# Sums of squares for an RMS norm: eight halves of tokens take another way, and one operand of a Strassen set is stored whole

## The chip, the cores and the metric

The kernel runs on one core of one Trainium2 chip. The metric is device time in microseconds (us) for one execution of the whole program; the time before is the median of three executions. TensorE (PE in the profile) multiplies matrices, VectorE (DVE), ScalarE (ACT) and GpSimd (POOL) do everything else, and SyncE (SP) issues nearly all the transfers (DMAs), in the order of its queue.

## The reference

Two layers over 1024 tokens of width 1024, in f32. Each layer is `h = h + mixer(rms_norm(h))` and then `h = h + conv_ffn(rms_norm(h))`; the first mixer is retention plus a gated delta rule, the second an RG-LRU; a last norm ends the program. What the change touches is the norm, which is computed five times:

```
def _rms(x):
    xf = x.astype(jnp.float32)
    return xf * lax.rsqrt(jnp.mean(xf * xf, axis=-1, keepdims=True) + EPS)
...
def conv_ffn(hn, w_up, conv_w, conv_b, w_down):
    up = causal_dwconv(hn @ w_up, conv_w) + conv_b
    gate, val = jnp.split(up, 2, axis=-1)
    return (jax.nn.silu(gate) * val) @ w_down
```

## The kernel before, in words

**Layout.** `h` lies in SBUF as eight tiles `H[m]` with 128 channels on the partitions and 1024 tokens along the free axis, and all work on it goes by halves of 512 tokens (n=0, n=1). The mean of squares of a token is therefore a sum over eight tiles and then over the 128 partitions.

**Products.** Weights and activations are split into a high and a low part in fp32r, and a product is three matmuls (lines 328 to 330: high by high, high by low, low by high). A weight quarter arrives by DMA into `raw` (7 buffers), is split by ACT (line 270, `whi`) and DVE (line 271, `wlo`) into a ring of 6 buffers, and a ring place comes free when TensorE has used it. So ACT and DVE can be up to 6 quarters ahead of TensorE, and no more.

**The norm.** `square_step` squares a half of each tile on ACT (line 416, the first one 407) and adds it to an accumulator on DVE (line 420); the eighth square is not added but kept beside it. `norm_tok` sums both over the partitions on TensorE: for each of the two arrays four f32 matmuls with one column of ones (line 433), in all eight, which leave one number per token, 128x4. Line 437 (DVE) scales it, line 438 (POOL) takes the power -0.5. `norm_row` turns it into a row on all partitions with four f32 matmuls of 128x128 (line 448); in three of the norms ACT copies that row from PSUM into `R` (line 451), in the others it is read from PSUM.

Where the halves are: the first norm stands at the start of the program (line 1518 on), while `x` is loaded. `down_x` (line 509) ends the first layer's FFN; its rows scale the projections of the RG-LRU (lines 388 and 1034). `down_pairs` (line 517) ends both mixers; as soon as a half is done, `pair_operands` builds from it, in small steps beside the next half's products, seven Strassen operands: scaled blocks (line 567, ACT), times the row (line 570, DVE), differences (594 and others), and high and low parts (583 and 587). For the second half these steps stand in a written order on DVE and ACT, and TensorE multiplies the first half's operands while they run (`pair_halves`). `final` (line 906) goes in three parts of 512, 256 and 256 tokens.

**The FFN's second matrix.** The hidden activations of 16 of the 22 pairs are multiplied by Strassen's seven products too, in two sets c=0 and c=1. `store_parts` writes four operands (0, 1, 3, 5) already split to `p_dram`, high and low, and three (2, 4, 6) whole to `s_dram`. `load_set` reads an operand back when TensorE has finished the one in its place: a split one with 8 DMAs straight to its place (line 831), a whole one with 4 DMAs into `t` (line 838), by way of six half-tile places that are used in turn, and is then split by ACT (line 840) and DVE (line 841). Set 0 is loaded while the last pair's products run.

**What sets the order.** The program is written in slots of three matmuls (`slot`, line 333); `steps` and `after` put an action so many slots later, so every `yield` of a generator is a slot. A scheduler then orders each engine's queue. Each engine runs its queue strictly in order: a waiting instruction holds everything behind it.

## Time and profile before

| what | before |
|---|---|
| median of 3 runs | 2199.09 us (2198.58 to 2200.04) |
| profiled execution, its own time | 2200.31 us |
| its span, first to last instruction | 2198.5 us |
| TensorE busy | 2176.4 us, 99% |
| VectorE busy | 1696.0 us, 77% |
| ScalarE busy | 1069.7 us, 49% |
| DMA bytes | 305.34 MB, 139 GB/s |

A busy TensorE is not one at its peak, since matmuls overlap: a 128x512 matmul shows 0.39 us, while the next starts 0.23 us later. So what an edit is worth on TensorE is read from start to start. An f32 matmul leaves two records, so the eight matmuls of a `norm_tok` show as x16.

### The profile page before, as it was taken

What the parts mean: (1) busy time and instruction counts of PE and PEld (TensorE: products, weight loads), DVE (VectorE), ACT (ScalarE), POOL (GpSimd) and SP (SyncE); (2) the same over time, 40 slices, a digit from 0 to 9 for tenths busy, and PEclk for the clock granted to TensorE, in tenths of its full rate; (3) what the DMA queues carried; (4) which work ended last, traced back from release to release, by engine and by line L of the source; (5) the groups of instructions that cost most, each with busy time, mean ns of one, the idle gap of its engine ahead of it and who ended that gap; (6) DMA issues with size and microseconds to landing.
All of it is one profiled execution on the core that took longest, in us unless ns stands there. A gap on an engine that the chain in (4) does not pass through costs nothing.

```text
span 2198.5 us, 29909 instructions
## 1 busy us (share of the span) xinstructions
PE 2176.4 (99%) x10844; PEld 1819.5 (83%) x10844; DVE 1696.0 (77%) x2576; ACT 1069.7 (49%) x1712; POOL 80.8 (4%) x73
## 2 busy tenths in 40 slices
PE   9999999999999999999999999999999999999998
PEld 8887888887888888887888888888888888878888
DVE  6988766446899988987865677778999889878644
ACT  5334433124565555554323476765655555544321
POOL 0100111200000000000000000000000000000001
PEclk9999999999999999999999999999999999999999
DMA  4243424125234544438546211242245445375542
GB/s 173 81 141 99 128 83 145 57 79 175 63 120 167 179 153 157 163 111 287 197 160 201 82 53 63 85 147 73 101 165 171 148 173 177 115 271 178 190 165 77
DMA packets 203300, 305.34 MB, mean 139 GB/s; under 512 B 31728, under 2 KB 91408, under 8 KB 203152
## 3 DMA queue, kind: packets, MB, share of 16 engines
q1 hardware_dynamic: 202720, 301.85, 40.7%
q8 instruction: 85, 1.39, 0.3%
q10 hardware_dynamic: 432, 1.58, 0.2%
q14 instruction: 63, 0.52, 0.1%
HBM read 212.63 MB, written 90.72 MB: 138 GB/s over the span
## 4 chain that ended last, share of the span: by engine, by line
PE 89%; DMA 4%; DVE 4%; issue 2%; ACT 1%; POOL 1%; SPq 0%; POOLq 0%; DVEq 0%; ACTq 0%
PE ps L328 27%; PE ps L330 27%; PE ps L329 27%; DMA t<-sf_dram 1%; DMA t<-y_dram 1%; PE pc L433 1%; DMA s<-pf_dram 1%; DMA h<-in_xT_dram 0%; DVE wlo L271 0%; PE pc L448 0%; DVE l L1273 0%; DVE l L1271 0%; PE pc L328 0%; PE pc L330 0%; PE pc L329 0%
## 5 line engine op out<-in xcount | busy, mean ns | idle before, releaser
L328 PE MATMUL ps<-s,whi 128*128 128x512 f32 (+1 forms) x2792 | 1091.0, 392 | 3.9 <-ACT s L840 1.8
L329 PE MATMUL ps<-s,whi 128*128 128x512 f32 (+1 forms) x2792 | 1084.5, 388 | 1.0 <-DVE s L841 0.7
L330 PE MATMUL ps<-s,wlo 128*128 128x512 f32 (+1 forms) x2792 | 1083.9, 388 | 0.0
L270 ACT CAST whi<-raw 128x512 fp32r<-128x512 f32 (+1 forms) x612 | 371.5, 613 | 659.1 <-PE ps L329 515.6
L328 PEld LDWEIGHTS ps<-s,whi 128*128 128x128 f32 x2792 | 524.9, 188 | 112.5 <-ACT s L840 3.1
L330 PEld LDWEIGHTS ps<-s,wlo 128*128 128x128 f32 x2792 | 524.7, 188 | 108.1 <-DVE wlo L271 0.3
L329 PEld LDWEIGHTS ps<-s,whi 128*128 128x128 f32 x2792 | 525.2, 188 | 107.3 <-DVE s L841 1.8
L271 DVE TENSOR_TENSOR wlo<-raw,whi 128x512 fp32r<-128x512 f32 (+1 forms) x612 | 412.9, 680 | 60.8 <-ACT whi L270 57.2
L774 DVE SCALAR_TENSOR_TENSOR t<-halo,cols,t 128x1024 f32<-128x1024 f32 x176 | 222.1, 1282 | 4.8 <-ACT t L772 3.5
L747 DVE TENSOR_TENSOR halo<-ps,kept 128x512 f32<-128x512 f32 (+1 forms) x138 | 92.2, 668 | 75.5 <-PE ps L330 74.2
L757 DVE TENSOR_TENSOR h<-ps,h 128x512 f32<-128x512 f32 x112 | 77.4, 691 | 82.2 <-PE ps L330 81.9
L772 ACT ACTIVATE t<-halo,cols 128x1024 f32<-128x1024 f32 x88 | 109.7, 1246 | 16.9 <-DVE halo L747 11.6
L742 ACT COPY kept<-ps 128x512 f32<-128x512 f32 (+1 forms) x138 | 77.0, 558 | 13.3 <-PE ps L330 11.2
L498 DVE TENSOR_TENSOR h<-ps,h 128x512 f32<-128x512 f32 (+1 forms) x72 | 45.3, 631 | 43.3 <-PE ps L330 43.3
L438 POOL TENSOR_TENSOR rtok<-rtok,npow 128x4 f32<-128x4 f32 (+1 forms) x11 | 11.2, 1016 | 1722.3 <-DVE rtok L437 1668.7
L857 DVE TENSOR_TENSOR t<-t 128x1024 f32<-128x1024 f32 x44 | 53.7, 1221 | 0.0
L797 ACT CAST t<-t 128x512 fp32r<-128x512 f32 x64 | 38.1, 620 | 32.0 <-DVE t L857 30.7
L852 ACT ACTIVATE t<-t 128x1024 f32<-128x1024 f32 x44 | 46.8, 1063 | 10.1 <-DVE t L774 10.0
L416 ACT ACTIVATE t<-h 128x512 f32<-128x512 f32 (+1 forms) x49 | 27.2, 562 | 46.3 <-DVE h L498 41.5
L840 ACT CAST s<-t 128x512 fp32r<-128x512 f32 x48 | 29.5, 621 | 38.4 <-DMA t<-sf_dram 34.0
L328 PE MATMUL ps<-s,s 128*128 128x256 f32 (+1 forms) x144 | 46.2, 321 | 0.0
L329 PE MATMUL ps<-s,s 128*128 128x256 f32 (+1 forms) x144 | 45.8, 318 | 0.0
(293 smaller groups left out, 2074.5 us busy)
## 6 DMA issues: line engine op xcount, KB each, us to landing
raw<-in_ffn_up_dram SPq DMA_DIRECT2D x176, 256.0 KB, 2.7
s<-pf_dram SPq DMA_DIRECT2D x128, 256.0 KB, 5.3
pf_dram<-t SPq DMA_DIRECT2D x64, 256.0 KB, 2.6
pf_dram<-lo SPq DMA_DIRECT2D x64, 256.0 KB, 2.5
sf_dram<-t SPq DMA_DIRECT2D x64, 256.0 KB, 2.2
t<-sf_dram SPq DMA_DIRECT2D x64, 256.0 KB, 5.0
raw<-in_ffn_w_dram SPq DMA_DIRECT2D x64, 256.0 KB, 2.9
raw<-in_mix_in_dram SPq DMA_DIRECT2D x62, 256.0 KB, 2.9
```

The lines of the kernel that those rows point to most:

```text
L270: self.nc.scalar.copy(hi[:, 0:w], raw[:, 0:w])
L271: eng.tensor_tensor(lo[:, 0:w], raw[:, 0:w], f32(hi[:, 0:w]), ALU.subtract)
L328: mm(ps, whi, xhi, start=start, stop=False)
L329: mm(ps, whi, xlo, start=False, stop=False)
L330: mm(ps, wlo, xhi, start=False, stop=stop)
L742: A.copy(kept[o], ps)
L747: V.tensor_tensor(dst(i, j), v(ps), v(kept[k]), ALU.add)
L757: V.tensor_tensor(h(*to[o]), ps.rearrange("p (h c) -> p h c", c=256), h(*to[o]), ALU.add)
L772: A.activation(t, buf[:, 2:2 + T], AF.Identity, scale=w(0), bias=self.col(f"ffn_cb{layer}", tile_i))
L774: V.scalar_tensor_tensor(t, buf[:, 2 + j:2 + j + T], w(j), t, ALU.mult, ALU.add)
L852: A.activation(tg, tg, AF.Silu)
L857: V.tensor_tensor(tg, tg, tv, ALU.mult)
```

## The change

1. With `st["whole"]`, the eighth square is added to the accumulator like the others, so `norm_tok` needs four matmuls for that half. This stands for both halves of the first norm, the second half of `down_x`, and the second part of `final` (256 tokens, two matmuls).
2. Four halves go by `norm_beside` and leave TensorE altogether: the first half of `down_x`, of both `down_pairs`, and the first part of `final`. DVE transposes the accumulator in blocks of 32x32 (`block_sums`) and reduces it to 128x16; four DMAs write these block sums to DRAM, one element at a time; a DMA reads them back by token, DVE adds the four, POOL takes the power, a DMA writes the row to DRAM and another reads it, broadcast, into `R`. All of these DMAs go by SP's queue.
3. In `pair_operands` the first half's row is now read from `R`; its steps start 16 slots after the last square, not 3, with no gap in them.
4. In the FFN, operand 5 of set 0 is stored whole (one DMA, straight from the activations) and split when it is loaded.

```diff
+        self.nsum = 0
...
-        if k == KT - 1:
+        if k == KT - 1 and not st.get("whole"):
             st["acc"].append(sq)
         else:
             nc.vector.tensor_tensor(st["acc"][0], st["acc"][0], sq, ALU.add)
+        if k == KT - 2:
+            st["free"] = sq
+
+    def block_sums(self, out, src, room):
+        self.nc.vector.transpose(room, src)
+        self.nc.vector.tensor_reduce(out, room.rearrange("p (b j) -> p b j", j=32), AX.X, ALU.add)
+
+    def norm_beside(self, st, n):
+        nc, V = self.nc, self.nc.vector
+        self.nsum += 1
+        sums = self.tc.dram_tile([4, HALF], F32, name=f"nsum_dram{self.nsum}")
+        row = self.tc.dram_tile([HALF], F32, name=f"nrow_dram{self.nsum}")
+        small = lambda name: self.sm.tile([P, 16], F32, tag=name, name=name, bufs=1)
+        b = small("nblk")
+        self.block_sums(b, st["acc"][0], st["free"])
+        for a in range(4):
+            nc.sync.dma_start(sums[a].rearrange("(b i) -> i b", i=32), b[32 * a:32 * a + 32, :])
+        x = small("ntok")
+        nc.sync.dma_start(x.rearrange("p (a c) -> p a c", a=4), sums.rearrange("a (p c) -> p a c", c=4))
+        r = self.sm.tile([P, 4], F32, tag="rtok", name="rtok")
+        V.tensor_reduce(r, x.rearrange("p (a c) -> p c a", a=4), AX.X, ALU.add)
+        V.tensor_scalar(r, r, 1.0 / D, EPS, ALU.mult, ALU.add)
+        nc.gpsimd.tensor_tensor(r, r, self.npow[:, 0:4], ALU.pow)
+        nc.sync.dma_start(row.rearrange("(p c) -> p c", c=4), r)
+        nc.sync.dma_start(self.R[:, n * HALF:(n + 1) * HALF], row.partition_broadcast(P))
+        self.has_row[n] = True
...
         def then(n, st, m, h):
+            st["whole"] = True
             self.square_step(st, m, self.norm_step(st, m, gain, n))
             if m == KT - 1:
-                self.steps((9, 7)[n], self.norm_rest(st, n, 3))
+                if n == 0:
+                    self.norm_beside(st, n)
+                else:
+                    self.steps(8, self.norm_rest(st, n, 3))
...
+            st["whole"] = n == 0
             self.square_step(st, m, h)
             if m == KT - 1:
+                if n == 0:
+                    self.norm_beside(st, n)
                 self.build[n] = self.pair_operands(st, n, gain, 4)
-                self.steps(3, self.build[n])
+                self.steps((16, 3)[n], self.build[n])
...
-        yield from self.norm_tok(st, wait=2)
+        if n == 0:
+            rows = self.R[:, 0:256], self.R[:, 256:HALF]
+        else:
+            yield from self.norm_tok(st, wait=2)
...
-        s_dram = self.tc.dram_tile([2, 4, 4, P, HALF], F32, name=f"sf_dram{layer}")
+        s_dram = self.tc.dram_tile([2, 5, 4, P, HALF], F32, name=f"sf_dram{layer}")
...
-        place = {1: 0, 4: 1, 2: 2, 6: 3}
-        whole = {0: 0, 1: 1, 3: 2, 5: 3}
+        place = {1: 0, 4: 1, 2: 2, 6: 3, 5: 4}
+        whole = [{0: 0, 1: 1, 3: 2}, {0: 0, 1: 1, 3: 2, 5: 3}]
...
-            store_split(5, v[:, :, 0], slice(HALF, T))
+            if 5 in whole[c]:
+                store_split(5, v[:, :, 0], slice(HALF, T))
+            else:
+                nc.sync.dma_start(halves(s_dram[c, place[5], k % 4]), v[:, :, 0])
...
-            st = {}
+            st = {"whole": t0 < 768}
...
-        s1 = part(512, 256, {2: [lambda: run(self.norm_tok(s0[0]))], 6: [lambda: run(self.norm_row(s0[0], 0))]})
+        self.norm_beside(s0[0], 0)
+        s1 = part(512, 256, {})
...
-            st, src = {}, {}
+            st, src = {"whole": True}, {}
```

**Where instructions move.** Line numbers of the changed kernel are higher: its 272, 400, 421 and 529 are the lines 271, 399, 420 and 498 of before, 468 and 479 are 437 and 448, and 608, 629 and 636 are 570, 587 and 594.

The first place is the first norm, on DVE, around the scaling of the first half's sums (`rtok<-pc`). Before:

```order
L420 TENSOR_TENSOR t<-t 128x512
L399 SCALAR_TENSOR_TENSOR s_96<-h_88,cols,s_96 128x512
L399 SCALAR_TENSOR_TENSOR s_96<-h_89,cols,s_96 128x512
L437 TENSOR_SCALAR rtok<-pc 128x4
L1177 TENSOR_SCALAR l_117<-l_117 128x4
L1601 TENSOR_SCALAR og<-cols 128x1
L399 SCALAR_TENSOR_TENSOR s_96<-h_90,cols,s_96 128x512
```

And now:

```order
L400 SCALAR_TENSOR_TENSOR s_96<-h_95,cols,s_96 128x512
L421 TENSOR_TENSOR t<-t 128x512
L468 TENSOR_SCALAR rtok<-pc 128x4
L421 TENSOR_TENSOR t<-t 128x512
L291 MEMSET wab 128x512 x2
L389 TENSOR_TENSOR halo_98<-ps,R 128x512
L389 TENSOR_TENSOR halo_99<-ps,R 128x512
L389 TENSOR_TENSOR l_117<-ps,R 128x512
L468 TENSOR_SCALAR rtok<-pc 128x4
```

The scaling of the first half has moved from behind the second half's second tile (`h_89`) to behind its last (`h_95`), and stands three rows ahead of the evacuations (`halo<-ps,R`) that need the row. On TensorE the row's matmuls have moved by as much: they now stand right ahead of the second half's `norm_tok`, and behind both come the first matmuls that need an evacuated bank.

The second place is the first `down_pairs`, behind the last tile (`h_95`) of its first half. DVE before:

```order
L498 TENSOR_TENSOR h_95<-ps,h_95 128x512
L271 TENSOR_TENSOR wlo<-raw,whi 128x512 x2
L437 TENSOR_SCALAR rtok<-pc 128x4
L498 TENSOR_TENSOR h_88<-ps,h_88 128x512
L271 TENSOR_TENSOR wlo<-raw,whi 128x512
L570 TENSOR_TENSOR t<-t,pc 128x1024 x2
L587 TENSOR_TENSOR s_4180<-t,s_4180 128x1024
```

DVE now, two rows further on (`h_88`, `h_89` and `h_90` are the first tiles of the second half):

```order
L529 TENSOR_TENSOR h_88<-ps,h_88 128x512
L272 TENSOR_TENSOR wlo<-raw,whi 128x512 x2
L446 TENSOR_REDUCE rtok<-ntok 128x4
L447 TENSOR_SCALAR rtok<-rtok 128x4
L529 TENSOR_TENSOR h_89<-ps,h_89 128x512
L272 TENSOR_TENSOR wlo<-raw,whi 128x512
L421 TENSOR_TENSOR halo_99<-halo_99 128x512
L272 TENSOR_TENSOR wlo<-raw,whi 128x512
L608 TENSOR_TENSOR t<-t,R 128x1024 x3
L629 TENSOR_TENSOR s_4174<-t,s_4174 128x1024
L529 TENSOR_TENSOR h_90<-ps,h_90 128x512
```

And SP's queue at the same place now; the rows other than 442 to 450 stood there before in the same order:

```order
L442 DMA nsum_dram_4777<-nblk 32x16x1 x4
L261 DMA raw<-in_mix_outb_dram 128x512
L261 DMA raw<-in_mix_outa_dram 128x512
L444 DMA ntok<-nsum_dram_4777 128x4x4
L261 DMA raw<-in_mix_outb_dram 128x512
L449 DMA nrow_dram_4778<-rtok 128x4
L302 DMA raw<-in_ffn_up_dram 128x512
L450 DMA R<-nrow_dram_4778 128x512
L302 DMA raw<-in_ffn_up_dram 128x512 x12
```

The build of the first half's operands, which began behind the addition to `h_88`, now begins behind that to `h_89`, and DVE stands twice for a DMA: at `rtok<-ntok` and at `t<-t,R`. Each DMA of the new chain has a weight load ahead of it in SP's queue.

The third place is SP's queue where set 0 is loaded. Before (the rows from the second to the sixth are operands 2, 3, 4, 5 and 6):

```order
L831 DMA s_4180<-pf_dram_5165 128x2x256 x6
L838 DMA t<-sf_dram_5164 128x512 x4
L831 DMA s_96<-pf_dram_5165 128x2x256 x8
L838 DMA t<-sf_dram_5164 128x512 x4
L831 DMA s_96<-pf_dram_5165 128x2x256 x8
L838 DMA t<-sf_dram_5164 128x512 x4
L301 DMA raw<-in_ffn_w_dram 128x512 x4
```

And now:

```order
L877 DMA s_4174<-pf_dram_5159 128x2x256 x6
L884 DMA t<-sf_dram_5158 128x512 x4
L877 DMA s_96<-pf_dram_5159 128x2x256 x8
L884 DMA t<-sf_dram_5158 128x512 x12
L302 DMA raw<-in_ffn_w_dram 128x512 x4
```

Operand 5's eight loads have become four, which go by the six places in `t` between those of operands 4 and 6, and four splits on ACT and on DVE have been added behind them.

More of the change, by code (lines that the diff above doesn't have):

```diff
@@ L140, in __init__ @@
         pad(self.perm, 104, "pad2")
-        pad(self.sm, 40, "pad3")
+        pad(self.sm, 24, "pad3")
         self.nhalo = 0
         self.npp = 0
+        self.nsum = 0
         self.lo_engine = nc.vector
@@ L575, in pair_operands @@
         scaled(b12, 0, 1)
-        yield from range(gap)
-        self.run(self.norm_row(st, apart=True))
-        rows = st["rows"]
+        if n == 1:
+            yield from range(gap)
+            self.run(self.norm_row(st, apart=True))
+            rows = st["rows"]
         place = lambda o: [self.operand(o)[:, n, e:e + 4, :] for e in (0, 4)]
@@ L799, in store_split @@
                 for e, t in enumerate((hi, lo)):
-                    nc.sync.dma_start(p_dram[c, whole[o], k % 4, e], f32(t[:, at]))
+                    nc.sync.dma_start(p_dram[c, whole[c][o], k % 4, e], f32(t[:, at]))
             store = lambda o, r: nc.sync.dma_start(s_dram[c, place[o], k % 4], r)
@@ L822, in store_parts @@
             store(6, t4)
-            store_split(5, v[:, :, 0], slice(HALF, T))
+            if 5 in whole[c]:
+                store_split(5, v[:, :, 0], slice(HALF, T))
+            else:
+                nc.sync.dma_start(halves(s_dram[c, place[5], k % 4]), v[:, :, 0])
         def load_set(c, o):
             x = self.operand(o)
-            if o in whole:
+            if o in whole[c]:
                 for k in range(4):
                     for e in range(2):
-                        nc.sync.dma_start(f32(x[:, :, 4 * e + k, :]), halves(p_dram[c, whole[o], k, e]))
+                        nc.sync.dma_start(f32(x[:, :, 4 * e + k, :]), halves(p_dram[c, whole[c][o], k, e]))
                 return
```

## The prediction, made before the changed kernel was run

> **What bounds the kernel now.** I read the page first, its busy times and the chain that ended last, then TensorE's timeline around the matmuls that the change removes, and then the windows in which TensorE waits.
>
> ```profile
> PE 2176.4 (99%) x10844; PEld 1819.5 (83%) x10844; DVE 1696.0 (77%) x2576; ACT 1069.7 (49%) x1712; POOL 80.8 (4%) x73
> PE 89%; DMA 4%; DVE 4%; issue 2%; ACT 1%; POOL 1%; SPq 0%; POOLq 0%; DVEq 0%; ACTq 0%
> 1215.67 0.39 PE L329 MATMUL ps<-s,whi 128*128 128x512 f32 x1
> 1215.90 0.39 PE L330 MATMUL ps<-s,wlo 128*128 128x512 f32 x1
> 1216.13 1.84 PE L433 MATMUL pc<-ones,t 128*128 128x1 f32 x16
> 1217.83 0.49 PE L328 MATMUL ps<-s,whi 128*128 128x512 f32 x1
> 1218.15 0.40 PE L329 MATMUL ps<-s,whi 128*128 128x512 f32 x1
> 1218.39 0.40 PE L330 MATMUL ps<-s,wlo 128*128 128x512 f32 x1
> ```
>
> TensorE carries 89% of the chain, and its matmuls start 0.23 us apart with nothing between. So whatever leaves its queue shortens the run by its own length, as long as no wait takes its place. What a `norm_tok` costs is read from start to start: 1217.83 - 1216.13 = 1.70 us, and the next two matmuls start 0.09 and 0.01 us later than the usual 0.23: 1.80 us for eight f32 matmuls.
>
> ```profile
> 550.95 0.94 PE L433 MATMUL pc<-ones,halo 128*128 128x1 f32 x8
> 551.76 0.49 PE L328 MATMUL ps<-s,whi 128*128 128x512 f32 x1
> 557.54 1.05 PE L448 MATMUL pc<-ident,rtok 128*128 128x128 f32 x8
> 558.35 0.48 PE L328 MATMUL ps<-s,whi 128*128 128x512 f32 x1
> ```
>
> Half a `norm_tok` is 0.81 + 0.10 = 0.91 us, and a row 0.81 + 0.09 = 0.90 us.
>
> **The change, part by part.** Four halves lose 1.80 + 0.90 = 2.70 us each, 10.8 us in all; three lose 0.90 and a quarter-sized one 0.40, 3.1 us in all. If nothing else moved, the program would be 13.9 us shorter. I go through the five places to see what of it is kept.
>
> *Both halves of `down_x`.* The first half's row isn't needed until the projections behind the second half, over 30 us later, so the DRAM way is covered. DVE's wait for the block sums holds back work there, but DVE is not full: 8.4 of 12 us (a window's columns are its length, the busy time of PE, weight loads, DVE, ACT and POOL, the clock, the DMA share and GB/s).
>
> ```profile
> 1204.00:1216.00 12.00, 12.00 (x55) 9.94 (x54) 8.37 (x15) 6.58 (x13) 0.00 (x0) 1.00 0.37 100
> 2140.00:2170.00 30.00, 30.00 (x216) 28.33 (x215) 10.80 (x20) 6.74 (x13) 2.81 (x3) 1.00 0.00 1
> ```
>
> I count the whole 2.70 + 0.90 = 3.6 us. *`final`* is as free: DVE works 10.8 of 30 us, DMA nothing. 2.70 + 0.40 = 3.1 us; what ends the program, the third part's norm, is not touched.
>
> *First norm.* Two halves of 0.90 us go. But the first half's scaling (468, before 437) now stands behind all of the second half's additions on DVE.
>
> ```profile
> 21.76 0.16 DVE L437 TENSOR_SCALAR rtok<-pc 128x4 f32<-128x4 f32 x1 [0.71 <-PE pc L433]
> 23.64 1.16 PE L448 MATMUL pc<-ident,rtok 128*128 128x128 f32 x8 [0.17 <-POOL rtok L438]
> 28.95 0.68 DVE L420 TENSOR_TENSOR t<-t 128x512 f32<-128x512 f32 x1
> 31.24 1.84 PE L433 MATMUL pc<-ones,t 128*128 128x1 f32 x16
> L451 ACT COPY R<-pc x2: 568/578/588, 27.7 to 41.7; 128x512 f32<-128x512 f32 x2
> L388 DVE TENSOR_TENSOR halo<-ps,R x4: 680/684/692, 29.6 to 46.4; 128x512 f32<-128x512 f32 x4
> ```
>
> DVE ends that addition at about 29.6 as before (one addition of 0.6 more, a wait of 0.71 less), and from the scaling to the row were 23.64 - 21.76 = 1.88 us: the row at 31.4. TensorE, which begins the second half's `norm_tok` at 31.24, would be there near 30.5 (six more matmuls ahead of it, 1.36, less 0.91, the old row's 0.90 and its wait of 0.34), so it waits 0.9 us; and since the evacuations need the row by way of ACT (0.58 us) and DVE (0.68 us), with only 0.8 us of `norm_tok` to cover them, it waits some 0.8 us again before it gets a bank. Of 1.8 us, and 0.34 us of the row's old wait, I keep 0.6; the bounds are 1.8 us won and 1 us lost.
>
> *First halves of the two `down_pairs`.* This is the place that decides. Before, the row came from TensorE, and DVE was full from 570 to 586 (the window in this fence is DVE's alone; its columns are length, busy, clock, DMA share, GB/s):
>
> ```profile
> 549.11 0.69 DVE L498 TENSOR_TENSOR h<-ps,h 128x512 f32<-128x512 f32 x1 [1.60 <-PE ps L330]
> 558.18 2.35 DVE L570 TENSOR_TENSOR t<-t,pc 128x1024 f32<-128x1024 f32 x2 [0.51 <-PE pc L448]
> 595.73 0.68 DVE L498 TENSOR_TENSOR h<-ps,h 128x512 f32<-128x512 f32 x1
> 597.87 0.95 PE L433 MATMUL pc<-ones,halo 128*128 128x1 f32 x8
> 570.00:586.00 16.00, 16.00 (x21) 1.00 0.18 54
> l_dram<-h SPq DMA_DIRECT2D x32, 16.0 KB, 1.5
> l<-t_dram SPq DMA_DIRECT2D x64, 16.0 KB, 1.9
> raw<-in_ffn_up_dram SPq DMA_DIRECT2D x176, 256.0 KB, 2.7
> L438 POOL TENSOR_TENSOR rtok<-rtok,npow 128x4 f32<-128x4 f32 x9 | 9.7, 1075 | 1707.4 <-DVE rtok L437 1653.9 <-DVE splq L1076 33.0 <-DVE og L1601 20.5
> L1354 DVE TENSOR_REDUCE ov<-l 128x4 f32<-128x512 f32 x16 | 11.0, 684 | 10.8 <-ACT l L1352 10.8
> L1246 SPq DMA_DIRECT2D l_dram<-h x32: 302/424/1571, 99.1 to 139.6; - x32
> DMA to landing us min/median/max: 1.4/1.5/4.2
> ```
>
> When is the new row in `R`? The last square is added near 551.3 (549.11, a square, an addition). No row shows a transpose; the reduce of the same 128x512 takes 0.68, and I take as much for each of the two: 552.7. Four issues of 512 single elements: 0.42 us for 128 pieces (`l_dram<-h`) is the lower bound; I take 0.6 each, 555.1. Landing 1.5 (upper bound 4.2), read back 1.9 and its issue, with a weight load between: 559. Two small DVE steps and the power (1.08): 560.7. Written behind another weight load, 1.5: 562.5. Broadcast behind a third, 2.7 as for another 256 KB: near 566. With every landing at 4.2 it is some 8 us later, with issues and landings at their least 3 us sooner.
>
> From there the changed order has on DVE 15 steps of 128x1024 (2.35 / 2 = 1.17 us) and 23 of 128x512 (0.6 us from start to start) before the addition to the second half's last tile: 15 x 1.17 + 23 x 0.6 = 31 us, so at 597 us, 1.3 later than the 595.73 of before. TensorE would have that tile ready at 592.7 (2.7 sooner), and its second-half `norm_tok` must wait. It had about 0.8 us in hand (597.87 against 595.73 and a square of 0.63), so it comes 0.5 to 0.7 us later than before, not 2.7 sooner: TensorE waits 3.4 us instead of working 2.7. I count 0.7 us lost in each, 1.4 in all. The bounds for each: 2.7 won, if the row comes 3 us sooner; 7 lost, if it comes 8 later.
>
> The wait has a second price. Where TensorE ran thin before, its clock was halved for a while:
>
> ```profile
> 1977.00:1979.00 2.00, 0.95 (x3) 0.48 (x3) 0.93 (x2) 0.86 (x2) 0.00 (x0) 1.00 1.05 403
> 1981.00:1983.00 2.00, 2.00 (x7) 1.52 (x6) 1.59 (x2) 2.00 (x4) 0.00 (x0) 0.50 0.09 34
> 1030.00:1040.00 10.00, 8.96 (x37) 6.09 (x35) 5.57 (x10) 3.90 (x7) 0.00 (x0) 1.00 1.07 392
> ```
>
> The third of these rows is a stretch nearly as thin that did not halve it. A clock of 0.50 for the 3 to 4 us seen there costs half of that, 1.7 us; I keep it in the range only. The Trainium skill's page "TensorE: Matmul & The Clock Gate", in its part 1 on the clock gate, says that the clock falls after an idle window of about 3.4 us. By that rule a wait of 3.4 us stands just at the edge, and the sum would be up to 3.4 us worse for both places; the row above disagrees in that the clock fell with three matmuls in two microseconds, without such an idle window.
>
> *Operand 5 of set 0, in both layers.* The windows from 1010 to 1050 show what it touches:
>
> ```profile
> 1010.00:1020.00 10.00, 10.00 (x46) 8.29 (x45) 6.56 (x10) 3.01 (x6) 0.00 (x0) 1.00 1.03 359
> 1040.00:1050.00 10.00, 9.56 (x38) 6.83 (x39) 9.29 (x14) 6.43 (x10) 0.00 (x0) 1.00 0.55 181
> 1027.64 5.17 SPq L831 DMA_DIRECT2D s<-pf_dram  x8
> 1033.65 1.96 SPq L838 DMA_DIRECT2D t<-sf_dram  x4
> 1038.50 1.92 ACT L840 CAST s<-t 128x512 fp32r<-128x512 f32 x3 [5.70 <-DMA t<-sf_dram]
> ```
>
> The DMA engines are full (1.03 to 1.07), and TensorE falls from 46 matmuls in 10 us to 37 and 38: 17 x 0.23 = 3.9 us. It waits for operand 6, whose loads stand behind operand 5's eight. Four loads instead of eight save SP 5.17 - 1.96 = 3.2 us and the engines 1 MB. But operand 6 can use the places in `t` only when the splits of operands 4 and 5 have freed them, which brings its last loads back to about 1035; they then land sooner, with less traffic. The added splits (4 x 0.6 on ACT and on DVE) lie in the time in which both wait (5.70 on ACT). I take half of the issue time, 1.6 us a layer, and 0.8 for a clock that is less likely halved in the second: 4.0 us. Bounds: all waits of both stretches gone with the halved clock (2 x 4.3, 8.6 us won), and 2 us lost where ACT's and DVE's added splits come last.
>
> *Sum:* 3.6 + 3.1 + 0.6 - 1.4 + 4.0 = 9.9 us less than the profiled execution's own 2200.3, which is 2190.4; the median shown is 1.2 us below that execution, so I predict 2189.2. A change of under 0.2% (4.4 us) can't be told from none here.
>
> **The rivals.** *All is kept.* If the row is in `R` by 563, `down_pairs` gains 2 x 2.7, the first norm 1.8, the loads 6: 3.6 + 3.1 + 1.8 + 5.4 + 6 = 19.9, so 2179. For it: the rows of 549.11 and 558.18 show DVE waits of 1.60 and 0.51 that the new order may fill. Against it: three weight loads stand between the DMAs of the chain. *The builds run late and the loads gain nothing:* 3 us lost in each `down_pairs`, 0 from operand 5: 3.6 + 3.1 + 0.6 - 6 = 1.3, so 2198. For it: DVE full to 586. *Slower:* the chain over DRAM is 8 us late in both `down_pairs`; DVE stands at `t<-t,R`, the weight splits queued behind it miss their turn in the ring of six, and TensorE runs dry there: 2 x 7 + 3.4 for the clock against 6.7 + 0.6 + 4, so 6.1 more: 2205. It decides once `R` comes after about 572. For it: landings of 4.2 us occur; against it: SP's transfers there are few (a DMA share of 0.18). *The change does nothing for the time,* because other work of TensorE would fill the gaps anyway: its share of 99% speaks against that; 2199.
>
> **How the numbers follow.** My forecast 0.55, with a range of its own from 2184 to 2195; all is kept 0.15; late builds 0.20; slower 0.05; nothing 0.05. The range that should hold the time 8 times in 10 runs from 2181, near the first rival, to 2197, near the second. Faster by over 0.2% means under 2194.7: 0.52 of the forecast, 0.15, and 0.09 of the late builds, in all 0.76; same 0.19; slower 0.05.
>
> **What would show it.** `down_x` and `final`: the matmuls gone, no new wait. First norm: TensorE waits for POOL ahead of the row and for DVE behind it, some 1.7 us. `down_pairs`: DVE waits for a DMA ahead of `t<-t,R`, ending near 566 less what was won earlier, and TensorE's second-half `norm_tok` waits some 3 us for ACT. Operand 6's casts start 1 to 2 us sooner relative to TensorE's products. I am wrong above all if the row is in `R` much sooner or later than 15 us behind the last square.

## The result

| | before | changed |
|---|---|---|
| median of the executions | 2199.57 us | 2219.84 us |
| lowest to highest | 2198.58 to 2200.04 | 2217.72 to 2224.95 |
| profiled execution, its own time | 2200.31 us | 2224.95 us |
| its span | 2198.5 us | 2223.2 us |

The changed kernel is slower: a ratio of 1.0096, with a 95% interval of 1.0078 to 1.0114, some 20 us where 10 us of gain were forecast. The profiled execution is the slowest of the four, 5 us above their median, so the stages below add up to 23.7 us, not to 20.

TensorE's row of the page, after, where before it stood at 2176.4 us with 10844 matmuls:

```profile
PE 2179.2 (98%) x10720; PEld 1817.6 (82%) x10720; DVE 1703.9 (77%) x2596; ACT 1068.4 (48%) x1710; POOL 81.4 (4%) x73
```

124 records of matmuls are gone, as meant, and the span grew all the same: the loss is waiting. Where it lies shows when the same matmul is looked up in both traces; the column "apart" is the later start less the earlier one, and what it grows by in a stage is what the stage lost.

| matmul at the end of | before, us | changed, us | apart | stage, measured | stage, forecast |
|---|---|---|---|---|---|
| first norm's first half | 19.55 | 19.70 | 0.15 | | |
| first norm | 44.90 | 44.37 | -0.52 | -0.7 | -0.6 |
| first half of the first `down_pairs` | 545.06 | 545.30 | 0.24 | +0.8 | 0 |
| first `down_pairs` | 629.96 | 640.59 | 10.63 | +10.4 | +0.7 |
| loads of set 0, first layer | 1059.95 | 1069.20 | 9.25 | -1.4 | -2.0 |
| `down_x` | 1280.02 | 1285.60 | 5.58 | -3.7 | -3.6 |
| second `down_pairs` | 1575.02 | 1591.65 | 16.63 | +11.1 | +0.7 |
| loads of set 0, second layer | 1990.09 | 2007.80 | 17.72 | +1.1 | -2.0 |
| `final`, up to its last row | 2191.08 | 2214.74 | 23.66 | +5.9 | -3.1 |

`down_x` and the first norm came out as forecast. The +0.8 in the third row is a stage in which nothing was changed; in the runs below the same stage lies between -0.2 and +3.7, so less than 1 us in a single trace says little. Most of the distance to the forecast lies in three terms: 20.1 us in the two `down_pairs`, 9.0 in `final`, 3.7 in the loads.

**The two `down_pairs`.** The chain of waits of the changed kernel, cut to the first place, with the short steps between the DMAs left out but for one (start, length, what):

```profile
554.42 9.13 DMA nsum_dram<-nblk
563.64 1.85 DMA ntok<-nsum_dram
565.73 0.18 DVE rtok L447
567.01 1.43 DMA nrow_dram<-rtok
568.46 4.84 DMA R<-nrow_dram
573.33 3.50 DVE t L608 x3
```

The first of these is the term that the forecast put at 1.5 us, with 4.2 as its upper bound. The group of all sixteen such DMAs says the same:

```profile
DMA to landing us min/median/max: 6.6/8.0/9.1
```

So the row was in `R` at 573.3, not at 566. VectorE's timeline shows the two places at which it stood, and where its build let it add the second half's last tile:

```profile
565.52 0.18 DVE L446 TENSOR_REDUCE rtok<-ntok 128x4 f32<-128x16 f32 x1 [6.84 <-DMA ntok<-nsum_dram]
573.33 3.50 DVE L608 TENSOR_TENSOR t<-t,R 128x1024 f32<-128x1024 f32 x3 [4.78 <-DMA R<-nrow_dram]
604.20 0.69 DVE L529 TENSOR_TENSOR h<-ps,h 128x512 f32<-128x512 f32 x1
```

From the row to that addition are 604.20 - 573.33 = 30.9 us; the forecast had counted 31. TensorE pays for it in five waits (brackets: the wait before the instruction, and for what):

```profile
580.95 0.50 PE L331 MATMUL ps<-s,wlo 128*128 128x512 f32 x1 [1.26 <-DVE wlo L272]
586.09 0.80 PE L331 MATMUL ps<-s,wlo 128*128 128x512 f32 x1 [2.13 <-DVE wlo L272]
591.30 0.50 PE L331 MATMUL ps<-s,wlo 128*128 128x512 f32 x1 [0.64 <-DVE wlo L272]
601.93 1.05 PE L464 MATMUL pc<-ones,halo 128*128 128x1 f32 x8 [1.57 <-DVE halo L421]
605.66 1.86 PE L464 MATMUL pc<-ones,halo 128*128 128x1 f32 x8 [1.39 <-ACT halo L417]
```

These are 7.0 us. The first three are weight splits that stood in VectorE's queue behind `t<-t,R`; the last two are the squares of the second half. And the waits have a second price. Windows (columns as in the prediction: length, busy PE, weight loads, DVE, ACT, POOL, clock, DMA share, GB/s):

```profile
579.20:582.60 3.40, 2.14 (x10) 1.45 (x9) 3.40 (x5) 2.09 (x4) 0.00 (x0) 1.00 0.15 40
582.60:586.00 3.40, 1.37 (x7) 0.79 (x5) 3.40 (x5) 2.29 (x4) 0.00 (x0) 1.00 0.10 37
586.00:589.40 3.40, 3.31 (x8) 2.66 (x9) 3.40 (x5) 3.40 (x8) 0.00 (x0) 0.50 0.24 77
603.08:613.32 10.24, 8.85 (x42) 8.56 (x42) 7.12 (x12) 2.82 (x7) 1.40 (x1) 0.50 0.34 104
```

Behind the thin window the clock is at half for the next 3.4 us, and again for 10.2 us from 603 on. The 7.0 us of waits less the 2.7 us of removed matmuls are 4.3 us. In the two stretches at half clock TensorE was busy for 3.3 and 8.9 us, and half of that, 6.1 us, is an estimate of what the clock cost. The two together are the 10.4 us, and the clock is the larger part.

**`final`.** VectorE and TensorE, in `final`:

```profile
2189.45 0.75 DVE L960 SCALAR_TENSOR_TENSOR h<-h,cols,R 128x512 f32<-128x512 f32 x1 [4.12 <-DMA R<-nrow_dram]
2197.04 1.02 PE L464 MATMUL pc<-ones,t 128*128 128x1 f32 x4 [5.75 <-DVE t L421]
```

The first part's scalings wait for the row, the second part's additions stand behind them in VectorE's queue, and TensorE waits for those. The forecast's "as free" was an average over 30 us. Here, too, the clock falls, while TensorE still waits:

```profile
2193.69:2203.93 10.24, 6.89 (x32) 6.89 (x33) 6.06 (x12) 1.99 (x5) 3.10 (x3) 0.50 0.40 150
```

A wait of 5.75 us, less 3.1 of removed work, and half of the 6.9 us make 6.1 by this estimate; 5.9 were lost.

**Operand 5.** SP's issues of the whole loads, and TensorE's and ACT's waits behind them:

```profile
1035.36 10.68 SPq L884 DMA_DIRECT2D t<-sf_dram x12
```

```profile
1052.76 0.50 PE L329 MATMUL ps<-s,whi 128*128 128x512 f32 x1 [0.88 <-ACT whi L271]
1052.08 0.62 ACT L271 CAST whi<-raw 128x512 fp32r<-128x512 f32 x1 [0.76 <-DMA raw<-in_ffn_w_dram]
```

Twelve loads take SP 10.7 us. Before, operands 4, 5 and 6 took from 1025.26 to 1033.65 + 1.96 = 1035.61, 10.4 us. The four issues that were saved are spent on waiting for places in `t`. The weight loads behind them are issued at 1046.09 in place of 1035.93, 10.2 us later, where TensorE itself is 10.4 us later: beside TensorE's products they come some 0.2 us sooner.

### The profile page after: what moved, and what is told of

Read it like the earlier page. It is cut to its first block, busy times and chain, and to the rows that moved or that the text cites. A ratio compares the mean times of both kernels' runs of the same rounds, so it can differ in the third digit from the quotient of the medians.

```text
span 2223.2 us, 29703 instructions
## 1 busy us (share of the span) xinstructions
PE 2179.2 (98%) x10720; PEld 1817.6 (82%) x10720; DVE 1703.9 (77%) x2596; ACT 1068.4 (48%) x1710; POOL 81.4 (4%) x73
## 4 chain that ended last, share of the span: by engine, by line
issue 41%; PE 38%; DVE 5%; DMA 3%; POOL 1%; ACT 0%; SPq 0%; POOLq 0%; DVEq 0%; ACTq 0%
PE ps L329 12%; PE ps L331 12%; PE ps L330 12%; DVE s L629 1%; DVE wlo L272 1%; DMA R<-nrow_dram 1%; DMA nsum_dram<-nblk 0%; DVE t L608 0%; DVE t L636 0%; DMA t<-y_dram 0%; DVE h L529 0%; PE pc L1457 0%; DVE halo L421 0%; DMA s<-pf_dram 0%; POOL ov L1406 0%
## 5 line engine op out<-in xcount | busy, mean ns | idle before, releaser
L886 ACT CAST s<-t 128x512 fp32r<-128x512 f32 x56 | 34.3, 621 | 32.4 <-DMA t<-sf_dram 27.7
```

## The experiments

"Before" is run beside each; its median there lies between 2200.2 and 2200.7 us. Ratios are to it.

### Each part alone

Only the two `down_pairs` by way of DRAM (the other parts undone):

```diff
-            st, src = {"whole": True}, {}
+            st, src = {}, {}
...
-            st["whole"] = True
...
-                if n == 0:
-                    self.norm_beside(st, n)
-                else:
-                    self.steps(8, self.norm_rest(st, n, 3))
+                self.steps((9, 7)[n], self.norm_rest(st, n, 3))
...
-            st = {"whole": t0 < 768}
+            st = {}
...
-        self.norm_beside(s0[0], 0)
-        s1 = part(512, 256, {})
+        s1 = part(512, 256, {2: [lambda: run(self.norm_tok(s0[0]))], 6: [lambda: run(self.norm_row(s0[0], 0))]})
...
-        whole = [{0: 0, 1: 1, 3: 2}, {0: 0, 1: 1, 3: 2, 5: 3}]
+        whole = [{0: 0, 1: 1, 3: 2, 5: 3}] * 2
```

> Of the change only the way by DRAM in the two down_pairs is left; the norms of down_x, final and the start, and operand 5, are as before. Theory A (the loss lies here: set side by side, the two traces drift apart by 9.3 us in the first down_pairs and by 11.1 us in the second): about 20 us slower than before, near 2220. Theory B (the forecast's sum, 0.7 lost in each): 1.4 us slower, not to be told from no change; the loss would then need the other parts beside it. Under A VectorE waits some 7 us for ntok and some 5 us for R in the first down_pairs.

Measured: 2220.65 us, ratio 1.0093 (1.0080 to 1.0107). Theory A. VectorE waits in the first place as in the changed kernel:

```profile
565.37 0.18 DVE L446 TENSOR_REDUCE rtok<-ntok 128x4 f32<-128x16 f32 x1 [6.00 <-DMA ntok<-nsum_dram]
573.07 3.50 DVE L604 TENSOR_TENSOR t<-t,R 128x1024 f32<-128x1024 f32 x3 [4.68 <-DMA R<-nrow_dram]
```

Only `final`, as the kernel before with these lines of the change and the functions that they call:

```diff
-            st = {}
+            st = {"whole": t0 < 768}
...
-        s1 = part(512, 256, {2: [lambda: run(self.norm_tok(s0[0]))], 6: [lambda: run(self.norm_row(s0[0], 0))]})
+        self.norm_beside(s0[0], 0)
+        s1 = part(512, 256, {})
```

> Before, with only the first part of final by way of DRAM and its second part summed whole. Theory A (the traces: TensorE waits 5.75 us for VectorE, which waits for R): 6 to 7 us slower, near 2206. Theory B (the forecast: nothing waits, 3.1 us of TensorE's work go): 3.1 us faster, 2196.5. A third, C, that the wait in the changed kernel comes from a clock or state left by the earlier stalls: faster here, too, and TensorE's wait for t gone.

Measured: 2208.90 us, ratio 1.0035 (1.0022 to 1.0048), 8.2 us slower; the profiled execution is one of the two fastest of six, 2205.38. Theory A; C falls, since nothing stalled ahead of it. TensorE's wait, at the same instruction:

```profile
2178.89 1.01 PE L464 MATMUL pc<-ones,t 128*128 128x1 f32 x4 [6.62 <-DVE t L421]
```

Only `down_x`:

```diff
+            st["whole"] = True
...
-                self.steps((9, 7)[n], self.norm_rest(st, n, 3))
+                if n == 0:
+                    self.norm_beside(st, n)
+                else:
+                    self.steps(8, self.norm_rest(st, n, 3))
```

> Before, with only down_x changed, its first half by way of DRAM, its second summed whole. The forecast and the traces agree on 3.6 to 3.7 us won: 2195.9. If the win depends on TensorE being late there from earlier stalls, it is less than 2 us.

Measured: 2196.55 us, ratio 0.9978 (0.9969 to 0.9987). As both said: in the traces the same matmul is 3.7 us earlier behind `down_x`. Here VectorE waits too, but TensorE doesn't wait for anything from 1200 to 1280 us:

```profile
1227.44 0.18 DVE L446 TENSOR_REDUCE rtok<-ntok 128x4 f32<-128x16 f32 x1 [5.30 <-DMA ntok<-nsum_dram]
```

Only operand 5:

```diff
-        whole = {0: 0, 1: 1, 3: 2, 5: 3}
+        whole = [{0: 0, 1: 1, 3: 2}, {0: 0, 1: 1, 3: 2, 5: 3}]
...
+                nc.sync.dma_start(halves(s_dram[c, place[5], k % 4]), v[:, :, 0])
```

> Before, with only operand 5 of set 0 stored whole. Theory A (the traces: 1.4 us won in the first layer, 1.1 lost in the second, where the twelve whole loads wait for their places and hold up the weight loads behind them on SP): within 1 us of before. Theory B (the forecast: loads are what TensorE waits for, 2.0 us a layer): 4.0 us faster, 2195.5.

Measured: 2217.53 us, ratio 1.0076 (1.0062 to 1.0090). Neither theory had that. TensorE's waits at the loads were shorter than before, but in both FFNs its matmuls stood 229.7 ns apart on average in place of 226.7: there were stretches in which every second one came 11 ns late. The small tiles of the DRAM way were missing in this kernel, while the padding beside them was still the changed kernel's 24 (the kernel before has 40), so that what is laid out behind them had moved by 128 bytes in each partition. Two runs tell the causes apart:

```diff
-        pad(self.sm, 24, "pad3")
+        pad(self.sm, 40, "pad3")
```

> As the run with operand 5 alone, with the padding of the small tiles back at 40, so that all of SBUF lies where it lay before; in the run without it the small tiles of the DRAM way were missing and the padding was 24, which moved what follows by 128 bytes a partition. There TensorE's matmuls stood 229.7 ns apart in place of 226.7 between 600 and 1000 us. Theory A (that is the placement's doing): 226.7 again and a time within 3 us of before, 2196 to 2200. Theory B (it is operand 5's doing): 2217 again.

And the kernel before with nothing but that number changed the other way, from 40 to 24:

> The kernel before with nothing but the padding of the small tiles at 24 in place of 40. Theory A (placement alone makes the matmuls 229.7 ns apart): 15 to 20 us slower, near 2217. Theory B (it is operand 5's doing): as before, 2199.

Measured: operand 5 with the padding 2198.29 us, ratio 0.9988 (0.9979 to 0.9996); the kernel before with the padding at 24, 2218.27 us in two executions, ratio 1.0077 (1.0059 to 1.0096). It is the placement. The same 100 us of the FFN, in the order before, operand 5 alone, before with 24, operand 5 with 40 (PE's count of matmuls in the first bracket):

```profile
700.00:800.00 100.00, 100.00 (x442) 82.83 (x442) 92.07 (x124) 57.20 (x86) 0.00 (x0) 1.00 0.47 162
```

```profile
700.00:800.00 100.00, 100.00 (x437) 81.73 (x436) 88.47 (x118) 55.24 (x80) 0.00 (x0) 1.00 0.45 151
```

```profile
700.00:800.00 100.00, 100.00 (x437) 81.69 (x436) 91.19 (x123) 57.22 (x85) 0.00 (x0) 1.00 0.46 161
```

```profile
700.00:800.00 100.00, 100.00 (x443) 82.87 (x442) 89.73 (x120) 55.54 (x82) 0.00 (x0) 1.00 0.44 151
```

Operand 5 itself wins: 2.0 us in the first layer and 1.1 in the second by the traces, 2.2 us by the medians. Not all of the 3.2 by the traces need be its own: in the runs that leave operand 5 as it was, the same two stages were 0 to 0.6 us shorter and 1.0 us shorter to 0.2 us longer than in before's trace, whose second layer has 3.4 us at half clock that the run with operand 5 doesn't have. The changed kernel keeps the old placement (its new small tiles fill what the padding gave up), and its matmuls stand 226.7 ns apart from 700 to 800 us, so none of its loss is from this.

### The landing of the block sums

If the landing is the term that failed, fewer and longer pieces must mend it. The block sums are written in the order in which they lie; the row is then in that order in `R` too, and is read with a stride:

```diff
-        for a in range(4):
-            nc.sync.dma_start(sums[a].rearrange("(b i) -> i b", i=32), b[32 * a:32 * a + 32, :])
+        nc.sync.dma_start(sums.rearrange("a (i b) -> (a i) b", b=16), b)
...
-            rows = self.R[:, 0:256], self.R[:, 256:HALF]
+            r = self.R[:, 0:HALF].rearrange("p (i b) -> p b i", b=16)
+            rows = r[:, 0:8, :], r[:, 8:16, :]
```

> As the run with only the two down_pairs changed, but the block sums go to DRAM in one DMA of 128 pieces of 64 bytes, in the order in which they lie, not in four DMAs of 512 single elements; the row then lies in R in that order, and VectorE reads it with a stride. Theory A (the landing of the element writes, 9.1 us where the forecast had 1.5, is the term that failed, and its other terms hold): R is read from near 566, and the program is as before to within 2 us, near 2201. Theory B (what TensorE waits for is VectorE's order, the two waits at ntok and R and the 31 us of build behind them, wherever R lands): still 10 us or more slower, over 2210. Theory C (the strided reading of R makes each multiplication by the row longer than 1.2 us, so nothing is won): over 2210 too, but with R early.

Measured: 2211.66 us, ratio 1.0051 (1.0038 to 1.0063). Nearly half of the loss is gone. The packets that the DMA engines moved while the block sums were written in the first place, in the changed kernel (10.7 us) and in this run (1.5 us):

```profile
DMA packets 2343, 0.44 MB, mean 41 GB/s; under 512 B 2134, under 2 KB 2134, under 8 KB 2343
```

```profile
DMA packets 144, 0.01 MB, mean 6 GB/s; under 512 B 144, under 2 KB 144, under 8 KB 144
```

The changed kernel's block sums are 2048 elements, this run's 128 pieces, so the counts fit one packet for each piece. The landing, VectorE and TensorE in this run:

```profile
DMA to landing us min/median/max: 1.4/1.4/1.4
```

```profile
565.74 3.83 DVE L608 TENSOR_TENSOR t<-t,R 128x1024 f32<-128x1024 f32 x2 [3.03 <-DMA R<-nrow_dram]
571.23 1.94 DVE L608 TENSOR_TENSOR t<-t,R 128x1024 f32<-128x1024 f32 x1
597.89 1.79 PE L466 MATMUL pc<-ones,halo 128*128 128x1 f32 x8 [2.14 <-DVE halo L421]
```

The edit also makes one DMA of four and changes the order in DRAM; these were not tried one by one. `R` came at 565.7, which is the forecast's 566, and still 5.7 us were lost in the first place and 5.9 in the second, not 0.7. Part of that is theory C: each of the four multiplications takes 1.9 us with the stride. Another part is the clock:

```profile
594.60:598.00 3.40, 1.26 (x11) 1.06 (x10) 3.40 (x7) 2.75 (x6) 0.00 (x0) 1.00 0.00 0
598.00:601.40 3.40, 3.16 (x14) 2.87 (x14) 3.40 (x7) 2.29 (x5) 0.00 (x0) 0.50 0.35 110
```

To take the stride away, ACT copies the row into place:

```diff
-        nc.sync.dma_start(self.R[:, n * HALF:(n + 1) * HALF], row.partition_broadcast(P))
+        apart = self.R[:, HALF:T]
+        nc.sync.dma_start(apart, row.partition_broadcast(P))
+        nc.scalar.copy(self.R[:, 0:HALF].rearrange("p (b i) -> p b i", i=32),
+                       apart.rearrange("p (i b) -> p b i", b=16))
```

> Both down_pairs by way of DRAM with the block sums written in pieces of 64 bytes; the row is broadcast into the free half of R and ACT copies it from there into place, so that VectorE's five multiplications by it read without a stride. In the run with the strided reading R came at 565.7, as the forecast had it, yet 11 us were lost: multiplications of 1.9 in place of 1.2 us, waits of TensorE of 2.1 and 1.2 us, and a clock at half for 10 us behind the longer one. Theory A (with the row in R by 567 and the multiplications at 1.2 us the forecast's sum holds): TensorE's wait for halo is under 1.5 us, the clock stays whole, and the time is within 2 us of before. Theory B (VectorE's queue behind the build holds the second half's squares back by 2 us or more wherever the row comes, and the clock falls each time): 2207 or more.

Measured: 2207.74 us, ratio 1.0034 (1.0022 to 1.0046). Theory B by the number. The rows say what of A holds:

```profile
567.28 2.36 DVE L612 TENSOR_TENSOR t<-t,R 128x1024 f32<-128x1024 f32 x2 [3.67 <-ACT R L455]
598.76 0.68 DVE L537 TENSOR_TENSOR h<-ps,h 128x512 f32<-128x512 f32 x1
596.49 1.05 PE L472 MATMUL pc<-ones,halo 128*128 128x1 f32 x8 [1.35 <-DVE halo L421]
600.32 1.86 PE L472 MATMUL pc<-ones,halo 128*128 128x1 f32 x8 [1.97 <-ACT halo L417]
```

The multiplications are at 1.2 us again, and VectorE reaches the last tile 31.5 us behind the row. TensorE waits 1.4 us for the sum of the first seven squares, then 2.0 us for the eighth, and behind them the clock is at half once more:

```profile
596.20:599.60 3.40, 1.87 (x14) 1.66 (x14) 3.40 (x7) 2.23 (x5) 0.00 (x0) 0.99 0.24 68
599.56:606.39 6.83, 6.07 (x28) 6.07 (x29) 3.75 (x7) 1.48 (x4) 1.40 (x1) 0.50 0.38 123
```

The loss is 3.1 us in the first place and 3.2 in the second. The two waits are 3.3 us, 0.6 more than the 2.7 us of removed matmuls; the half clock cost some 3.0 us, half of the 6.07 us in which TensorE was busy. That makes 3.6 us, and a later wait of 0.8 us that before has is gone. So nearly all of this loss is the clock, by this estimate.

The last try was to free the chain of the weight loads in SP's queue, by issuing its DMAs from GpSimd (`nc.gpsimd.dma_start` in place of `nc.sync.dma_start` in `norm_beside`):

> As the run in which ACT copies the row into place, with the four DMAs of the way by DRAM on GpSimd's queue, where no weight load stands ahead of them. In the two runs before, the second half's last tile was added on VectorE 30.9 and 31.5 us behind the arrival of R (573.3 to 604.2, 567.3 to 598.8), as the forecast counted (31 us). Theory A (TensorE's loss is set by when R comes): each us by which R comes before 567.3 is a us less lost in each down_pairs until, near 564, nothing is lost; so if the row comes 2 us sooner, 2202 to 2204. Theory B (the weight loads in the queue are not what delays it, or another queue's issues cost as much): R at 567 or later and 2207 or more.

Measured: 2215.69 us, ratio 1.0064 (1.0050 to 1.0078). Theory B: the row came later. The chain of waits of this run:

```profile
556.42 3.15 DMA nsum_dram<-nblk
559.87 2.68 DMA ntok<-nsum_dram
564.78 3.26 DMA nrow_dram<-rtok
568.33 5.07 DMA R<-nrow_dram
```

From SP's queue, in the run before it, the four took 1.43, 2.40, 3.16 and 3.33 us: the first and the last took 1.7 us longer from GpSimd, the other two 0.1 and 0.3. As an experiment on the row's time it served all the same. "Lag" is from the start of the addition to the first half's last tile to VectorE's first `t<-t,R`; "lost" is how much further the traces are apart behind the place than ahead of it:

| kernel | lag, first place | lost | lag, second place | lost |
|---|---|---|---|---|
| ACT copies the row | 16.7 | 3.1 | 16.8 | 3.2 |
| DMAs from GpSimd | 22.0 | 7.7 | 21.0 | 6.4 |
| `down_pairs` alone | 23.0 | 8.2 | 25.4 | 11.9 |
| the changed kernel | 24.0 | 10.4 | 24.5 | 11.1 |
| read with a stride | 16.1 | 5.7 | 15.7 | 5.9 |

From 16.7 to 25.4 us the loss grows by 8.8 us, one for one between the ends, with the runs between them up to 1.2 us below that line. Continued downwards, the line reaches zero near 13.6 us; no run came that early, so that end is only drawn on. The run with the stride lies some 3 us above the line. Its multiplications, four and not five as the expectation has it, take 0.7 us more each, which fits; but its clock was also at half for 10.2 us and not 6.8, so the stride's share is not shown.

### `final` with an earlier row

The same two mends for `final` alone (written whole and read with a stride, and copied by ACT):

> As the run with only final changed, with the block sums written in 64-byte pieces and R read with a stride by VectorE and GpSimd. Theory A (the late row is what stops VectorE, and with it TensorE): R comes about 8 us sooner, TensorE's wait of 5 us for t is gone, and the 3.1 us of removed work are won: 2197. Theory B (VectorE's scalings stand ahead of the second part's evacuations whenever the row comes): still slower than before by 3 us or more.

> Only final by way of DRAM, block sums in pieces of 64 bytes, and ACT copies the row into place, so that the scalings read without a stride. Theory A (the strided scalings, up to 2.4 us each where they took 1.3 before, made the wait of 3.9 us): the wait falls to 2 us or less, the clock stays whole, and 1 to 2 us are won against before, 2198.5. Theory B (TensorE's matmuls gone bring it to the second part's sums before VectorE has them, whatever the scalings take): the wait stays over 3 us, and nothing is won or up to 3 us lost.

Measured: 2203.61 us, ratio 1.0015 (1.0006 to 1.0025), and 2199.89 us, ratio 0.9998 (0.9989 to 1.0006). In the second run:

```profile
2168.41 3.59 DVE L957 SCALAR_TENSOR_TENSOR h<-h,cols,R 128x512 f32<-128x512 f32 x2 [2.93 <-ACT R L455]
2177.15 0.61 PE L472 MATMUL pc<-ones,t 128*128 128x1 f32 x4 [2.31 <-DVE t L421]
```

Before, the row came by way of TensorE and ACT:

```profile
2167.64 0.59 ACT L451 COPY R<-pc 128x512 f32<-128x512 f32 x1
```

The row is now there at 2168.4; before, ACT's copy of it ended at 2167.6 + 0.6 = 2168.2. With the row no later than before, TensorE comes sooner to the second part's sums and waits 2.3 us for VectorE. What was removed came back as a wait: here the end is set by the row and VectorE's scalings, not by TensorE. Theory A forecast a wait of 2 us or less, which is nearly so, but also a gain and a whole clock; there was no gain, and the clock was at half for 3.4 us behind the wait.

### The parts that win

`down_x`, operand 5, and in `final` only the second part summed whole; then with the first norm summed whole too:

```diff
-            st = {"whole": t0 < 768}
+            st = {"whole": t0 == 512}
```

> The parts that won alone: down_x as in the change and operand 5 of set 0 whole, and in final only the second part summed whole (0.4 us less on TensorE). down_pairs and the first norm are as before. If the parts add up: 4.0 (3.6 by the rows) and 2.3 to 2.7 and 0.4, so 6.5 to 7 us faster, 2193.5. If operand 5's gain was chance between placements: 4 us faster.

> As the one before it, with both halves of the first norm summed whole too. By the forecast's step 0.6 us faster than that; by the trace of the changed kernel, where the waits before and behind the row take 1.2 of 1.8 us and those of the start another part, no difference; if the late row holds up the first evacuations further, slower by up to 1 us.

Measured: 2195.02 us, ratio 0.9975 (0.9967 to 0.9984), and 2195.86 us, ratio 0.9983 (0.9971 to 0.9995). The parts add up to 5.5 us of the 6.5 expected. For the first norm the two intervals overlap: no gain to be seen; its two waits are there, 0.56 us for GpSimd's power and 0.61 us for the evacuation. In this trace the clock is at half for 3.4 us behind them, and the stage lost 0.9 us where the changed kernel's won 0.7.

Last, in both `down_pairs` the first half's eighth square added on VectorE, the rest left on TensorE:

```diff
+            st["whole"] = n == 0
             self.square_step(st, m, h)
```

> The parts that won (down_x, operand 5, the second part of final), and in both down_pairs the eighth square of the first half added on VectorE like the others, the sums and the row still on TensorE. TensorE has 0.9 us less in each, VectorE 0.6 more ahead of the row. If the row's arrival sets the end of VectorE's build, 0.6 us later in each: 1 us slower than without it, 2196; if VectorE has that in hand: 1.8 us faster, 2193.

Measured: 2192.76 us, ratio 0.9964 (0.9951 to 0.9976), the lowest median of all, 7.5 us below before. Its interval overlaps that of the run without this step (0.9967 to 0.9984), so the medians alone don't show the step's gain; in the traces each `down_pairs` is 0.7 us shorter, of the 0.9 us that were removed. The row doesn't come later, it comes sooner: before, the second four of `norm_tok`'s matmuls started 2.3 us behind the first four, and they are gone. VectorE's first multiplication by the row and the last tile:

```profile
556.12 2.34 DVE L606 TENSOR_TENSOR t<-t,pc 128x1024 f32<-128x1024 f32 x2
594.52 0.69 DVE L529 TENSOR_TENSOR h<-ps,h 128x512 f32<-128x512 f32 x1 [0.29 <-PE ps L331]
```

The lag is 556.12 - 548.92 = 7.2 us, where before had 558.18 - 549.11 = 9.1; and at the last tile VectorE now waits for TensorE.

## Why the prediction was wrong, step by step

- **When is the new row in `R`?** This step failed, in one term: the landing of the block sums, put at 1.5 us, the median of DMAs of 128 pieces, with 4.2, the longest of them, as its upper bound. It was 8.0 us, 9.1 in the first place. So the row came 21.8 us behind the last square and not 15, which the prediction itself had named as the sign of being wrong. The rows used were of other shapes: none of them moves 512 single elements. With one DMA of 128 pieces the landing was 1.4 us and the row came at 565.7. The other terms were right in their sum only: from the landing to the row the forecast had 9.4 us, the changed kernel 9.8, and the run with one DMA 11.0, of which the write of the row alone took 3.4 where 1.5 was put. The Trainium skill's page "DMA: Bandwidth & Descriptors", section "Rules for kernel authors", says that a transfer whose last dimension is strided becomes one descriptor per element. The runs agree, with 2134 small packets against 144 and a landing of 8.0 us against 1.4 for the same bytes.
- **What VectorE does from there (31 us).** Right: 30.9 us in the changed kernel, 31.5 with ACT's copy.
- **0.7 us lost in each place.** Wrong even with the row near the forecast's time: 3.1 and 3.2 us. The step that failed here is the clock, which was kept in the range and put at nothing in the sum. The wait was right in size: 3.4 us were forecast for one wait, and the run with ACT's copy has 1.4 us for the seven squares and 2.0 for the eighth, 0.6 us more than the removed 2.7. The half clock of 6.8 us behind them is the rest. The bound "7 lost, if it comes 8 later" was of the right kind but left the clock out, too: with the row 7 us later, 10.4 and 11.1 were lost.
- **The clock.** In each trace the clock changes only in steps of 3.4 us or a multiple of that. No idle window is needed for it to fall: TensorE was busy for 1.26 to 1.87 us of the 3.4 ahead of the halved windows shown here, and its single waits were 1.4 to 2.1 us. But neither number is a threshold. In the run with the DMAs from GpSimd, two windows just as thin left the clock whole in the first `down_pairs`, and it fell only at 606:

```profile
585.54:588.95 3.41, 1.66 (x8) 1.37 (x8) 3.41 (x4) 3.32 (x6) 0.00 (x0) 1.00 0.11 36
588.95:592.37 3.42, 1.87 (x9) 1.23 (x8) 3.42 (x5) 3.42 (x7) 0.00 (x0) 1.00 0.11 41
```

With the first norm summed whole on top of the parts that win, it fell behind a window with 2.5 us of work, at 34.0. What decides stays open. The row that the prediction held against a halved clock, 8.96 us busy of 10, was not nearly as thin as the 0.95 of 2 beside it. The Trainium skill's page "TensorE: Matmul & The Clock Gate", part 1, names an idle window of about 3.4 us as what halves the clock; the runs agree on the 3.4 us and not on the idleness. By the windows, 3.4 to 10 us at half clock cost 1.7 to 5 us, an estimate.
- **`final` is free.** Wrong: 5.9 us lost, not 3.1 won. The step put the wait for the row at nothing because VectorE had room in a window of 30 us, which averaged over the stretch in which it scales the first part; TensorE waited 5.75 us there. And with the row as early as before, nothing was won, since what follows the row sets the end there.
- **`down_x`.** Right to 0.1 us, in the changed kernel and alone, by the traces. In the traces of the last two runs with it the stage won only 2.5 and 2.3 us, with a wait of TensorE of 0.6 us for GpSimd's power that the others don't have.
- **First norm.** The waits are 0.59 and 0.61 us where 0.9 and 0.8 were said. Set side by side, the stage won 0.7; put on top of the other parts it won nothing that can be measured.
- **Operand 5.** Right in direction, too large: 4.0 forecast, 3.2 by the traces of the run alone, 2.2 by its medians. The half of SP's issue time was not saved (10.7 us for the twelve against 10.4). In the changed kernel the second layer lost 1.1 us: its clock was at half for 3.4 us there, but so was before's, and the waits between the matmuls grew from 1.4 to 2.3 us.
- **The slower rival** had the right mechanism (the chain late, VectorE standing at `t<-t,R`, weight splits behind it, the clock's price on top) and 2205. Its own condition, `R` after about 572, was met at 573.3; its chance of 0.05 hung on the 4.2 us as the longest landing. It left out `final`.

What stays open: the split of the 3.1 us at a lag of 16.7 into clock and waits is an estimate, since no run had one without the other; what makes the clock fall; and whether a row by way of DRAM within 14 us would win in `down_pairs`.

## What to carry to other kernels

Count the pieces of a transfer, not its bytes or issues: rearrange so that pieces are long where a wait hangs on it, and put the permutation into a copy on an idle engine. Work taken off a full engine is won only where that engine is what the next step waits for; look at the few us behind the removed work, not at an average, and ask which in-order queue will now be waited for. A part that hides its new waits (`down_x`) may be kept alone when the same edit costs elsewhere. And put a price on the clock behind a wait of TensorE in the sum, not only in the range: in `down_pairs` and `final` it cost more than the waits less the removed work.

## What the runs showed of the hardware

- The small tiles taking 128 bytes less of each partition made TensorE's matmuls in the FFN some 1.1% slower (437 for 442 in 100 us) at a full clock, 18 us in the program. Which operand's place does it was not tried.
- The clock was halved for 3.4 us or a multiple of that behind windows of 3.4 us in which TensorE was busy for 1.0 to 2.5 us; other windows with 1.7 and 1.9 us left it whole.
- 8 KB written to DRAM as single elements by four DMAs landed after 6.6 to 9.1 us, as 128 pieces by one DMA after 1.4. Two weight loads of 256 KB issued while the elements were on their way landed after 8.6 and 8.7 us; one beside the 128 pieces, after 2.6.
- VectorE read `R` with a stride of 16 elements at 1.9 us for 128x1024, against 1.2 without.
- The write of the block sums in 128 pieces took 3.0 and 3.1 us from issue to landing from GpSimd's queue, and 1.4 from SP's.
